# A planner that writes the order of one kernel: its price list and three of its waiting times are changed

## Chip, cores and metric

The kernel runs on one core of a Trainium2 chip. The metric is device time of one execution in microseconds (us), lower is better. TensorE (PE), VectorE (DVE), ScalarE (ACT) and GpSimd (POOL) each work through their own list of instructions in the order in which the program wrote them; SyncE (SP) issues nearly all DMAs, in order as well.

## What is computed

Two macaron layers over 256 latent tokens and 256 context tokens of width 1024, all in float32. Cut to what matters:

```python
for i in range(2):                                  # layer 0: DeltaNet mixer, layer 1: window attention
    mx = silu(c) @ ada_w[i] + ada_b[i]              # nine vectors of 1024 for the latent tokens
    mc = silu(c_ctx) @ ada_w[i] + ada_b[i]          # nine for the context tokens
    x   = x   + 0.5 * gate * swiglu(rms_norm(x) * scale + shift)       # FFN 1, width 2816
    ctx = ctx + 0.5 * gate * swiglu(rms_norm(ctx) * scale + shift)
    x   = x   + gate * mixer(norm(x), norm(ctx))    # chunked gated DeltaNet in two directions, or attention
    ctx = ctx + gate * mixer(...)                   # not in the last layer
    x   = x   + 0.5 * gate * swiglu(norm(x))        # FFN 2; for ctx not in the last layer
    ctx = ctx + 0.5 * gate * swiglu(norm(ctx))
```

Shift, scale and gate are the nine vectors `mx`, `mc`, called the ada vectors below.

## The kernel before

Activations lie transposed: features on partitions, 512 tokens (context in columns 0 to 255, latent in 256 to 511) on the free axis. A weight block of 128x128 times an activation block is done as three matmuls (`mm3`): high part times high part, high times low, low times high, since every float32 is split into a rounded part and a remainder. ACT and DVE (or POOL) make these splits from weights that SP loads into the rings `raw` and `ub` of two tiles each. A ring `u` of 76 tiles of 128x512 holds all else: a tile is given back after its last use in the program.

An FFN has three parts of 6, 8 and 8 hidden blocks (`self.parts`): pairs of products, then `out_blocks`, which adds the gated result to `X` block by block. The last part of an FFN computes the last four blocks in two halves, context columns first, and each half is followed by `norm_half`: a sum of squares over partitions on PE (`rstd`, a matmul with `ones`), then eight chunks of the next input `H` by DVE, ACT and POOL (`h_chunks`). The next stage begins with the context halves of four units, so that the latent norm can run meanwhile.

The ada vectors are a background task (`ada_gen`): a vector is 16 steps, each of which loads 256 KB of `ada_w` and multiplies and adds it into accumulators on DVE, ACT and POOL; after the 16th, four matmuls with `ones1` sum over partitions, ACT copies the result, PE transposes it. Tiles are loaded three steps ahead. During DeltaNet the task is paused (`ada_pause`, set before the last `out_blocks` of the first FFN, cleared when the norm after DeltaNet is made). `need(l, v)` runs the task at once if a vector is asked for that isn't there.

In DeltaNet (`deltanet`) PE works through projections, while `dn_prep`, `dn_solve` (a triangular solve on DVE), `dn_kq` (sums of squares of the queries, then products of keys and queries) and `dn_chain` (eight recurrent steps per head) run as tasks, heads 0 to 3 first, then 4 to 7. For the second group `dn_kq` stores keys and queries to DRAM, and `dn_group` loads them again when the first group is through.

**The planner.** The order on all engines is written while the program is built, by `Sched`. It keeps a clock that each matmul moves on by its assumed duration (`mm`, `tr`), estimated times at which DVE, ACT and POOL come free (`note`), and for each piece of a tile when it will be ready. A task is a generator: what it yields is the time in ns until it wants to go on, and `yield self.at(tile)` means "when the tile is ready by the estimate". What a task then issues stands at that place in every engine's list. The estimates are used only for the order: on the chip an instruction waits until its inputs are truly there, and with it all that stands behind it on its engine.

Of the kernel before, what the change touches and what calls it, by code (L numbers as in the profile page):

```python
# [68 lines left out]
class Sched:  # L69
# [3 lines left out]
    def __init__(self):  # L73
        self.clock = 0.0
        self.tasks = []
        self.busy = False
        self.free = {"vector": 0.0, "scalar": 0.0, "gpsimd": 0.0, "dma": 0.0}
        self.ready = {}
        self.slot = 0.0

    @staticmethod
# [15 lines left out]
    def note(self, eng, ins, outs, n, extra):  # L97

        t = max(self.free[eng], self.when(*ins))
        a, b, c = {"vector": (70.0, 1.04, 65.0), "scalar": (60.0, 0.84, 90.0), "gpsimd": (80.0, 2.15, 0.0)}[eng]  # L100
        self.free[eng] = t + a + b * n + c * extra
        for o in outs:
            self.mark(o, self.free[eng] + 150.0)

# [109 lines left out]
class Kernel:  # L214
    PACE = 2450.0
    Z0 = 1
# [32 lines left out]
    def at(self, *aps):  # L249

        return max(0.0, self.s.when(*aps) - self.s.clock)


    def act(self, **kw):
# [13 lines left out]
    def mm(self, out, lhsT, rhs, start=True, stop=True, tp=None, ns=None):  # L268
        kw = {} if tp is None else {"tile_position": tp}
        if ns is None:  # L270
            n = 1
            for d in rhs.shape[1:]:
                n *= d
            m = lhsT.shape[-1]
            if lhsT.dtype == F32R:
                ns = max(107.0, n / 2.4)
            else:
                ns = max(214.0 if m > 64 else 135.0, 4 * n / 2.4)
        self.s.product([lhsT, rhs], out, ns)
        self.nc.tensor.matmul(out, lhsT, rhs, start=start, stop=stop, **kw)  # L280
        self.s.tick(ns)

    def tr(self, out, in_, k=128):
        self.s.product([in_], out, 107.0)
        self.nc.tensor.transpose(out, in_, self.ident[:k, :k])  # L285
        self.s.tick(107)

# [390 lines left out]
    def ada_gen(self, todo, pace):  # L678
# [12 lines left out]
        def ahead(i):  # L691
            if i < len(steps) and i not in tiles and not (self.ada_pause and steps[i][3:] == (0, 0)):
                if not self.ada_pause or i - 1 in tiles or i - 1 == cur[0]:
                    fetch(i)
# [6 lines left out]
        for i, (l, v, conds, h, k) in enumerate(steps):  # L701
# [30 lines left out]
            p = c = None  # L732
            yield (1800.0 if i < 16 else pace) - (self.s.clock - t0)
            if h == 1 and k == 7:
                yield self.at(*acc.values())
                n = 32 * 2 * len(conds)
# [6 lines left out]
                self.act(out=sb[0:n, :], in_=ps[0:n, :], func=AF.Copy)  # L743
                yield self.at(sb)
                p2 = self.cht()
# [106 lines left out]
    def norm_half(self, hf, sq, l, slot):  # L852
        self.need(l, 3 * slot)
        self.need(l, 3 * slot + 1)
        sl = CTX if hf == "c" else LAT
        yield self.at(self.acc[:, sl]) + self.margin
        yield from self.rstd(sl, sq)
        yield self.at(self.rs[:, sl])
        yield from self.h_chunks(hf, l, slot, range(8), 300)
        if hf == "x":  # L860
            self.tables("silu")
            self.norming = self.urgent = self.lo_mix = False
            if (l, slot) == (0, 2):
                self.ada_pause = False

# [228 lines left out]
    def ffn(self, l, j, sl, nxt, start=False):  # L1094
        v = 8 if j else 2
        for pi, (p0, n) in enumerate(self.parts):
            self.G = ([], [])
            if pi == 0:
                if start:
# [56 lines left out]
    def dn_consts(self):  # L1156
        nc, a = self.nc, self.a
        self.dnc = [self.u(), self.u()]
        for i in range(2):
            nc.sync.dma_start(out=self.dnc[i], in_=a["dnc"][:, 512 * i:512 * i + 512])  # L1160
        d0, d1 = self.dnc
        self.tri = [d0[:, 0:128], d0[:, 128:256]]
        self.bones = d0[:, 256:384]
        self.tric = [d0[:, 384:448], d0[:, 448:512]]
        self.hsel = [d1[:, 0:128], d1[:, 128:256]]
        self.maskr = self.const([128, 2, 64], "maskr", F32R)
        self.identr = self.const([128, 128], "identr", F32R)
        self.fwd, self.bwd = d1[:, 384:385], d1[:, 385:386]
        rows = self.u()
# [323 lines left out]
    def dn_kq(self, g):  # L1493

        while any(4 * g + i not in self.qsq for i in range(4)):
            yield 500
        yield self.at(*[self.qsq[4 * g + i] for i in range(4)])
        yield from self.dn_ss(self.qsq, g, self.lnq)
# [43 lines left out]
    def dn_chain(self, h):  # L1542
# [8 lines left out]
        for s, (q, e) in enumerate(self.STEPS):  # L1551
# [9 lines left out]
            if s:  # L1561
                for i in range(2):
                    self.mm(ps[half[i], 0:128], kT[:, c0[i]:c0[i] + 64], S[:, e ^ i, :], ns=135)
                yield self.at(ps[:, 0:128])
# [18 lines left out]
            if s:  # L1583
                for i in range(2):
                    self.mm(po[half[i], 0:128], qT[:, c0[i]:c0[i] + 64], S[:, e ^ i, :], ns=135)
            self.mm(po[:, 128:256], KQ, w)
# [286 lines left out]
    def att_worker(self, todo):  # L1873
        nc = self.nc
        while todo:
# [44 lines left out]
            for k in range(4):  # L1920
                for par in range(2):
                    self.mm(po[64 * par:64 * par + 64, 0:128], self.aV[c][:, 128 * k + 64 * par:128 * k + 64 * par + 64],
                            PT[par][:, 128 * k:128 * k + 128], start=(k == 0), stop=(k == 3), ns=135)
            hi, lo = self.OH[0][u][:, qs], self.OH[1][u][:, qs]
# [38 lines left out]
    def run(self, upto=None):  # L1963
# [5 lines left out]
        self.margin = 300.0  # L1969
        self.lo_pool = self.ada_pause = self.norming = self.urgent = self.lo_mix = False  # L1970
        self.plan_weights()
# [61 lines left out]
```

## Time and profile before

| what | value |
|---|---|
| median of 3 runs | 1926.43 us (1924.85 to 1928.46) |
| the profiled execution | 1927.54 us, span of its instructions 1925.8 us |
| PE busy | 1866.0 us, 97% of the span |
| DVE, ACT, POOL busy | 1283.1, 965.7, 649.2 us |
| DMA | 271.76 MB, mean 141 GB/s |

Rows of the trace give times from the start of the span. A line of code is that of a helper for nearly all instructions (L280 is the matmul in `mm`, L285 the transpose, L184 the wrapper of the other engines), so tiles tell them apart: `mm` is a PSUM tile, `u`, `ub`, `raw`, `big` are tiles of the rings, `ones` the matrix of ones of either sum.

### The profile page before, as it was taken

To read this page: it belongs to the slowest core of one execution; us is meant where nothing else is said; L and a number is where in the kernel's file an instruction comes from. 1 tells how busy PE (TensorE), PEld (TensorE's weight loads), DVE (VectorE), ACT (ScalarE), POOL (GpSimd) and SP (SyncE) were. 2 spreads that over 40 slices of the span, in tenths; PEclk is the share of its full clock that TensorE was granted. 3 is DMA by queue.
4 is the path that set the end of the run, shared out by engine and by line. 5 is a ranking of instruction groups with operands and counts; after the bars stand their busy time and mean duration, and the time that the engine had idled before them with its cause. 6 is when DMAs were issued, how large, how long until landed. Compare 5 with 4: busy or idle time off the path is not lost.

```text
span 1925.8 us, 28970 instructions
## 1 busy us (share of the span) xinstructions
PE 1866.0 (97%) x10719; PEld 1527.8 (79%) x10719; DVE 1283.1 (67%) x2121; ACT 965.7 (50%) x2106; POOL 649.2 (34%) x597
## 2 busy tenths in 40 slices
PE   8999999999999999999999999999999999899998
PEld 5878788887777766787888888888888889678887
DVE  4897878855986975478888655743333345966665
ACT  4545535457466555465454344641322348865653
POOL 3344434453545535354444224420000047330000
PEclk8999999999999999999999999999999999999999
DMA  9655554423222252444555555433223325124761
GB/s 293 209 198 201 181 186 170 139 63 108 90 68 88 67 182 83 145 169 152 197 191 197 186 172 173 153 126 109 88 88 109 113 69 123 47 67 148 235 197 66
DMA packets 238421, 271.76 MB, mean 141 GB/s; under 512 B 12184, under 2 KB 188592, under 8 KB 238280
## 3 DMA queue, kind: packets, MB, share of 16 engines
q1 hardware_dynamic: 237415, 269.22, 43.0%
q8 instruction: 84, 1.38, 0.3%
q10 hardware_dynamic: 720, 0.59, 0.1%
q14 instruction: 58, 0.47, 0.1%
q0 software_dynamic: 144, 0.11, 0.0%
HBM read 259.39 MB, written 10.49 MB: 140 GB/s over the span
## 4 chain that ended last, share of the span: by engine, by line
PE 56%; DVE 7%; ACT 3%; issue 3%; POOL 1%; DMA 1%; POOLq 0%; DVEq 0%; ACTq 0%; SPq 0%
PE mm L280 55%; DVE u L184 6%; ACT u L184 3%; PE mm L285 1%; POOL u L184 1%; DVE st L184 0%; DVE big L184 0%; DMA u<-ZD 0%; DMA u<-XD 0%; ACT L184 0%; DVE ub L184 0%; POOLq L184 0%; ACT sc L184 0%; DVEq L184 0%; ACTq L184 0%
## 5 line engine op out<-in xcount | busy, mean ns | idle before, releaser
L280 PE MATMUL mm<-u 128*128 128x512 f32 (+4 forms) x9496 | 1782.0, 353 | 22.4 <-POOL u L184 8.3
L280 PEld LDWEIGHTS mm<-u 128*128 128x128 f32 (+1 forms) x9496 | 1459.3, 184 | 325.8 <-issue 42.3
L184 POOL TENSOR_TENSOR u<-u 128x512 f32<-128x512 f32 (+4 forms) x389 | 430.2, 1112 | 909.8 <-ACT u L184 859.0
L184 ACT ACTIVATE u<-u 128x512 fp32r<-128x512 f32 (+8 forms) x361 | 171.2, 485 | 441.9 <-DVE u L184 420.3
L184 ACT ACTIVATE u<-mm 128x128 f32<-128x128 f32 (+3 forms) x382 | 151.9, 412 | 291.7 <-PE mm L280 223.1
L184 DVE TENSOR_TENSOR u<-raw,u 128x512 fp32r<-128x512 f32 (+2 forms) x270 | 218.6, 851 | 65.1 <-ACT u L184 65.0
L184 DVE SCALAR_TENSOR_TENSOR u<-u,cc 128x512 f32<-128x512 f32 x196 | 229.2, 1170 | 4.2 <-DMA u<-in_ada_w 1.0
L184 DVE TENSOR_TENSOR u<-ub,u 128x512 fp32r<-128x512 f32 x252 | 198.1, 830 | 26.7 <-ACT u L184 26.4
L184 ACT ACTIVATE u<-raw 128x512 fp32r<-128x512 f32 (+1 forms) x372 | 205.8, 607 | 14.6 <-DMA raw<-in_ffn_w 10.3
L184 ACT ACTIVATE u<-u,cc 128x512 f32<-128x512 f32 x224 | 151.9, 711 | 84.9 <-DMA u<-in_ada_w 71.7
L184 POOL TENSOR_TENSOR u<-raw,u 128x512 fp32r<-128x512 f32 x98 | 130.1, 1351 | 141.5 <-ACT u L184 121.8
L184 ACT ACTIVATE u<-ub 128x512 fp32r<-128x512 f32 (+1 forms) x282 | 155.9, 608 | 20.2 <-DVE u L184 8.2
L184 DVE TENSOR_TENSOR u<-u,mm 128x512 f32<-128x512 f32 x66 | 45.2, 685 | 164.9 <-PE mm L280 156.7
L184 DVE TENSOR_TENSOR u<-u 128x512 fp32r<-128x512 f32 (+5 forms) x155 | 96.9, 626 | 64.9 <-ACT u L184 61.9
L184 DVE SCALAR_TENSOR_TENSOR u<-mm,mod,u 128x256 f32<-128x256 f32 x168 | 74.5, 477 | 93.8 <-PE mm L280 93.6
L184 DVE SCALAR_TENSOR_TENSOR u<-u,mod 128x256 f32<-128x256 f32 (+1 forms) x140 | 88.3, 683 | 23.9 <-ACT u L184 23.6
L184 ACT ACTIVATE u<-u,mod 128x256 fp32r<-128x256 f32 (+1 forms) x124 | 56.0, 501 | 52.7 <-DVE u L184 52.3
L184 DVE SCALAR_TENSOR_TENSOR u<-mm,cw,u 128x510 f32<-128x510 f32 (+1 forms) x96 | 71.3, 743 | 9.6 <-ACT u L184 7.9
L285 PE MATMUL mm<-ident,u 128*128 128x128 f32 (+3 forms) x361 | 55.3, 289 | 13.7 <-DVE u L184 7.1
L184 DVE TENSOR_TENSOR u<-mm,u 128x256 f32<-128x256 f32 (+2 forms) x102 | 41.6, 419 | 36.5 <-PE mm L280 16.6
L285 PEld LDWEIGHTS mm<-ident,u 128*128 128x128 f32 (+3 forms) x361 | 43.7, 149 | 25.2 <-ACT u L184 6.0
L280 PE MATMUL mm<-u,ones 128*32 128x512 f32 (+2 forms) x172 | 37.3, 546 | 13.0 <-DVE u L184 8.9
(116 smaller groups left out, 587.0 us busy)
## 6 DMA issues: line engine op xcount, KB each, us to landing
u<-in_ada_w SPq DMA_DIRECT2D x256, 256.0 KB, 5.7
ub<-in_ffn_w SPq DMA_DIRECT2D x60, 1024.0 KB, 5.3
raw<-in_ffn_w SPq DMA_DIRECT2D x58, 1024.0 KB, 5.3
raw<-in_dn_w_in SPq DMA_DIRECT2D x16, 1024.0 KB, 5.7
ub<-in_ada_w SPq DMA_DIRECT2D x12, 512.0 KB, 7.2
ub<-in_ffn_w SPq DMA_DIRECT2D x6, 768.0 KB, 4.7
raw<-in_ffn_w SPq DMA_DIRECT2D x6, 768.0 KB, 4.8
raw<-in_dn_w_out SPq DMA_DIRECT2D x4, 1024.0 KB, 5.8
```

The costliest lines, as they stand in the source:

```text
L184: r = f(*a, **k)
L280: self.nc.tensor.matmul(out, lhsT, rhs, start=start, stop=stop, **kw)
L285: self.nc.tensor.transpose(out, in_, self.ident[:k, :k])
```

## The change

The price list of the planner gets other numbers (`Sched.note`, `mm`, `tr`), a vector operation with two inputs is lengthened by 45% of the time for which POOL is still busy by the estimate, and a matmul after a switch to fewer than 128 rows or columns gets 95 ns more (`form`). A new wait `spare` is `at` plus 2500 ns; it stands before the sums and the transposes of an ada vector and before the sums in `dn_kq`. The latent half of `norm_half` waits 1200 ns after its estimate where it waited 300. `PACE`, the time of an ada step, goes from 2450 to 2650 ns (1800 to 1900 for the first vector). From the last part of the first FFN on, `ada_hold` keeps the first tiles of a new vector from being loaded ahead. The constants of DeltaNet, two `u` tiles, are split: what is used to the end goes to a tile of its own (`keep`), the rest is last used in `dn_gates`.

```diff
+        self.split = False
+    def form(self, split):
+        was, self.split = self.split, split
+        return 95.0 if split and not was else 0.0
...
-        self.free[eng] = t + a + b * n + c * extra
+        took = a + b * n + c * extra
+        if eng == "vector":
+            both = len(ins) > 1 and not any(i.tensor.name.startswith("mm") for i in ins)
+            if both:
+                took += 0.45 * max(0.0, min(took, self.free["gpsimd"] - t))
+        self.free[eng] = t + took
         for o in outs:
-            self.mark(o, self.free[eng] + 150.0)
+            self.mark(o, self.free[eng] + 200.0)
...
-    PACE = 2450.0
+    PACE = 2650.0
...
+    def spare(self, *aps):
+        return max(0.0, self.s.when(*aps) + 2500.0 - self.s.clock)
...
             if lhsT.dtype == F32R:
-                ns = max(107.0, n / 2.4)
+                ns = n / 2.4 + m / 9.4
             else:
-                ns = max(214.0 if m > 64 else 135.0, 4 * n / 2.4)
+                ns = (214.0 if m > 64 else 107.0) * max(1.0, n / 128) + 12.0
+        ns += self.s.form(lhsT.shape[0] < 128 or lhsT.shape[-1] < 128)
...
-        self.s.product([in_], out, 107.0)
+        ns = 109.0 + self.s.form(in_.shape[0] < 128)
+        self.s.product([in_], out, ns)
...
-            if i < len(steps) and i not in tiles and not (self.ada_pause and steps[i][3:] == (0, 0)):
+            if i < len(steps) and i not in tiles and not ((self.ada_pause or self.ada_hold) and steps[i][3:] == (0, 0)):
...
-            yield (1800.0 if i < 16 else pace) - (self.s.clock - t0)
+            yield (1900.0 if i < 16 else pace) - (self.s.clock - t0)
             if h == 1 and k == 7:
-                yield self.at(*acc.values())
+                yield self.spare(*acc.values())
...
-                yield self.at(sb)
+                yield self.spare(sb)
...
-        yield self.at(self.acc[:, sl]) + self.margin
+        yield self.at(self.acc[:, sl]) + (self.margin if hf == "c" else 1200.0)
...
-                self.ada_pause = False
+                self.ada_pause = self.ada_hold = False
...
+            if pi == 2 and (l, j) == (0, 0):
+                self.ada_hold = True
...
-        self.dnc = [self.u(), self.u()]
-        for i in range(2):
-            nc.sync.dma_start(out=self.dnc[i], in_=a["dnc"][:, 512 * i:512 * i + 512])
-        d0, d1 = self.dnc
+        d0, d1 = self.u(), self.u()
+        nc.sync.dma_start(out=d0[:, 0:256], in_=a["dnc"][:, 0:256])
+        nc.sync.dma_start(out=d1[:, 0:384], in_=a["dnc"][:, 512:896])
+        keep = self.const([128, 258], "keep")
+        nc.sync.dma_start(out=keep[:, 0:256], in_=a["dnc"][:, 256:512])
+        nc.sync.dma_start(out=keep[:, 256:258], in_=a["dnc"][:, 896:898])
...
-        yield self.at(*[self.qsq[4 * g + i] for i in range(4)])
+        yield self.spare(*[self.qsq[4 * g + i] for i in range(4)])
...
-                    self.mm(ps[half[i], 0:128], kT[:, c0[i]:c0[i] + 64], S[:, e ^ i, :], ns=135)
+                    self.mm(ps[half[i], 0:128], kT[:, c0[i]:c0[i] + 64], S[:, e ^ i, :], ns=110)
...
```

Two more matmuls with `ns=135` get 110, and the views `tri`, `bones`, `tric`, `hsel`, `fwd`, `bwd` point to the new places.

## Rows read from the trace of the kernel before

**Rows 1.** Busy time by stretch; us, PE, PEld, DVE, ACT, POOL, PE clock, DMA.

```profile
45.00:365.00 320.00, 319.62 (x1454) 256.39 (x1453) 270.60 (x320) 156.23 (x278) 142.70 (x95) 1.00 0.57 192
...
895.00:1195.00 300.00, 300.00 (x1384) 243.53 (x1382) 220.63 (x282) 133.97 (x237) 112.51 (x77) 1.00 0.54 185
...
1570.00:1735.00 165.00, 149.47 (x1185) 132.35 (x1185) 113.39 (x274) 125.21 (x293) 81.28 (x77) 0.99 0.27 71
```

**Rows 2.** Waits of PE between 411 and 792 us: total us, times, longest.

```profile
PE mm L280 <- ACT u L184: 7.2, 7, 3.3
PE mm L280 <- POOL u L184: 3.6, 5, 1.0
PE mm L280 <- DVE u L184: 3.3, 7, 0.8
```

**Rows 3.** PE in order of time: start us, us, what, idle time before it.

```profile
83.75 21.01 PE L280 MATMUL mm<-u 128*128 128x512 f32 x92
104.69 1.31 PE L280 MATMUL mm<-u,ones 128*32 128x512 f32 x8
107.51 0.66 PE L285 MATMUL mm<-ident,u 128*128 128x128 f32 x4 [0.38 <-ACT u L184]
...
388.80 1.00 PE L280 MATMUL mm<-u 128*128 128x256 f32 x7
389.72 1.04 PE L280 MATMUL mm<-u,ones 128*32 128x512 f32 x2
392.97 1.06 PE L280 MATMUL mm<-u,ones 128*32 128x512 f32 x6 [2.20 <-DVE u L184]
...
396.00 0.66 PE L285 MATMUL mm<-ident,u 128*128 128x128 f32 x4 [0.83 <-ACT u L184]
...
894.15 1.06 PE L280 MATMUL mm<-u,ones 128*32 128x512 f32 x6 [1.28 <-DVE u L184]
```

**Rows 4.** PE in order of time at the first sums of `dn_kq`.

```profile
516.81 1.06 PE L280 MATMUL mm<-u,ones 128*32 128x512 f32 x6
521.15 1.23 PE L280 MATMUL mm<-u,ones 128*32 128x512 f32 x2 [3.28 <-ACT u L184]
```

**Rows 5.** Busy time by stretch where the clock was low; columns as in rows 1.

```profile
521.90:525.30 3.40, 3.40 (x11) 2.18 (x12) 3.33 (x8) 1.90 (x3) 0.00 (x0) 0.50 0.01 2
750.60:757.40 6.80, 6.80 (x40) 5.10 (x38) 4.40 (x15) 2.99 (x14) 4.35 (x8) 0.50 0.60 204
```

**Rows 6.** PE in order of time at the norms after DeltaNet and before attention.

```profile
831.55 0.67 PE L280 MATMUL mm<-u,ones 128*128 128x256 f32 x2 [1.79 <-DVE u L184]
...
832.77 11.62 PE L280 MATMUL mm<-u 128*128 128x256 f32 x94
844.88 5.29 PE L280 MATMUL mm<-u 128*128 128x256 f32 x42 [0.50 <-POOL u L184]
...
1585.16 0.67 PE L280 MATMUL mm<-u,ones 128*128 128x256 f32 x2 [1.78 <-DVE u L184]
```

**Rows 7.** DVE by shape, 60 to 365 us: count, busy us, mean ns.

```profile
L184 DVE TENSOR_TENSOR u<-raw,u 128x512 fp32r<-128x512 f32 x54 | 53.7, 1034 | 2.9 <-ACT u L184 2.9
```

**Rows 8.** The same, 1740 to 1900 us, where POOL does nothing.

```profile
L184 DVE TENSOR_TENSOR u<-raw,u 128x512 fp32r<-128x512 f32 x55 | 35.9, 687 | 38.4 <-ACT u L184 38.4
```

**Rows 9.** PE between the two groups of DeltaNet.

```profile
683.49 1.07 PE L280 MATMUL mm<-u,ones 128*32 128x512 f32 x8
...
694.49 0.75 PE L280 MATMUL mm<-ub,u 32*32 32x32 f32 x64 [0.48 <-ACT u L184]
...
748.97 10.06 PE L280 MATMUL mm<-u 64*128 64x128 f32 x64 [1.63 <-ACT u L184]
```

**Rows 10.** SP's queue there: start us, us, what it issued.

```profile
686.84 0.42 SPq L184 DMA_DIRECT2D QD<-u  x1
```

**Rows 11.** SP and DVE in order of time around the first vector after DeltaNet.

```profile
838.39 2.92 SPq L184 DMA_DIRECT2D u<-in_ada_w  x6
...
908.17 0.86 DVE L184 SCALAR_TENSOR_TENSOR u<-mm,mod,u 128x256 f32<-128x256 f32 x2
```

More of the change, by code (lines that the diff above doesn't have):

```diff
@@ L283, in tr @@
     def tr(self, out, in_, k=128):
-        self.s.product([in_], out, 107.0)
+        ns = 109.0 + self.s.form(in_.shape[0] < 128)
+        self.s.product([in_], out, ns)
         self.nc.tensor.transpose(out, in_, self.ident[:k, :k])
-        self.s.tick(107)
+        self.s.tick(ns)
     def mm3(self, ps, w, h, nk, sl=ALL, ks=None, start=True, stop=True):
@@ L1157, in dn_consts @@
         nc, a = self.nc, self.a
-        self.dnc = [self.u(), self.u()]
-        for i in range(2):
-            nc.sync.dma_start(out=self.dnc[i], in_=a["dnc"][:, 512 * i:512 * i + 512])
-        d0, d1 = self.dnc
+        d0, d1 = self.u(), self.u()
[4 more added lines that the diff above has]
+        nc.sync.dma_start(out=keep[:, 256:258], in_=a["dnc"][:, 896:898])
         self.tri = [d0[:, 0:128], d0[:, 128:256]]
-        self.bones = d0[:, 256:384]
-        self.tric = [d0[:, 384:448], d0[:, 448:512]]
+        self.bones = keep[:, 0:128]
+        self.tric = [keep[:, 128:192], keep[:, 192:256]]
         self.hsel = [d1[:, 0:128], d1[:, 128:256]]
@@ L1167, in dn_consts @@
         self.identr = self.const([128, 128], "identr", F32R)
-        self.fwd, self.bwd = d1[:, 384:385], d1[:, 385:386]
+        self.fwd, self.bwd = keep[:, 256:257], keep[:, 257:258]
         rows = self.u()
@@ L1584, in dn_chain @@
                 for i in range(2):
-                    self.mm(po[half[i], 0:128], qT[:, c0[i]:c0[i] + 64], S[:, e ^ i, :], ns=135)
+                    self.mm(po[half[i], 0:128], qT[:, c0[i]:c0[i] + 64], S[:, e ^ i, :], ns=110)
             self.mm(po[:, 128:256], KQ, w)
@@ L1922, in att_worker @@
                     self.mm(po[64 * par:64 * par + 64, 0:128], self.aV[c][:, 128 * k + 64 * par:128 * k + 64 * par + 64],
-                            PT[par][:, 128 * k:128 * k + 128], start=(k == 0), stop=(k == 3), ns=135)
+                            PT[par][:, 128 * k:128 * k + 128], start=(k == 0), stop=(k == 3), ns=110)
             hi, lo = self.OH[0][u][:, qs], self.OH[1][u][:, qs]
@@ L1969, in run @@
         self.margin = 300.0
-        self.lo_pool = self.ada_pause = self.norming = self.urgent = self.lo_mix = False
+        self.lo_pool = self.ada_pause = self.ada_hold = self.norming = self.urgent = self.lo_mix = False
         self.plan_weights()
```

## The prediction

> **What bounds the kernel now.** I read the busy time by stretch first. In the FFN stretches from 45 to 365 and from 895 to 1195 us PE is busy for 319.6 of 320 and 300.0 of 300 us [rows 1]; the order of time shows 92 matmuls of 512 columns in 21.01 us, 228 ns each [rows 3]. No order makes these stretches shorter: the number of matmuls doesn't change. So the change can win only where PE stands still: in DeltaNet, in the joints between stages and in attention, where PE lacks 15.5 of 165 us [rows 1]. The waits of PE say for what: between 411 and 792 us 7.2 us for ACT, 3.6 for POOL and 3.3 for DVE [rows 2]. Then I looked up each place in the order of time. What the reader is to see there: PE's list is worked off in order, so an instruction put too early holds up everything behind it, though the matmuls behind it need nothing from it. That is what a planner that is too hopeful does.
>
> How hopeful it is, one pair of rows shows. The same subtraction (two inputs in SBUF, 128x512) takes 1034 ns on average while POOL has work [rows 7] and 687 ns in the last FFN, where POOL does nothing [rows 8]. The planner before reckons 70 + 1.04 x 512 = 602 ns for both. Its 512-column matmul is 213 ns, 228 on the chip.
>
> **Term A, sums of the ada vectors.** Four times PE waits at the end of a vector: 0.38 us before a transpose, 2.20 and 0.83 us at 390 and 396, 1.28 us at 894 [rows 3]; together 4.69 us. The other vectors show no such wait. Behind the waiting matmul stand the matmuls of the FFN, which are ready; put off, the sums let them go first, and the work in front of them is free. At 390 the first sums ran at 389.72 and the rest at 392.97 [rows 3]: 3.25 us too early, against 2.5 us of delay. Of that wait I leave 0.4 us and count **4.3 us**. Bounds: nothing, if the sums meet another late accumulator, and 4.7.
>
> How much of the contention the new price list sees is a second question. For one subtraction it adds up to 0.45 x 602 = 271 ns; the rows differ by 1034 - 687 = 347 ns on average, and that average holds operations that POOL left alone. The Trainium skill (SBUF — State Buffer, Who interferes with whom) says that a vector operation with two SBUF inputs and a GpSimd operation that reads SBUF exclude each other for a whole instruction. By that rule the loser pays the whole rest of the other's instruction and not 45% of it, and one more late operation of some 0.3 us would stay at each of the four places, so that A would be about 3.1 us; the sum goes without it.
>
> **Term B, the sums of the queries.** At 516.81 us three quarters of the sums run, and the last quarter waits until 521.15, 3.28 us idle, for ACT behind a DVE that is busy with the solver [rows 4]. It is 4.3 us too early; the delay is 2.5, and dearer DVE operations and 50 ns more per result push it further. I leave 1.0 us and count 2.3. Right behind that wait the granted clock is 0.50, that is 1.2 GHz, from 521.9 to 525.3 [rows 5]: the 3.4 us would hold the same work in 1.7 at 2.4 GHz. I count them, since PE then has no wait of 3 us there: B is **4.0 us**. Bounds 0 (the clock falls anyway and the wait is as long) and 5.0. Nobody waits for these sums soon: the products of `dn_kq` also wait for the decay factors.
>
> **Term C, the latent norm.** At 831.55 PE waits 1.79 us for the last accumulation [rows 6], and 1.78 us at the joint before attention [rows 6]. Put off by 900 ns more, PE would do context matmuls meanwhile. But these are done too soon anyway: after the norm's sums PE has 11.62 us of them, and at 844.88 it waits another 0.50 us for the last chunk of `H` from POOL [rows 6]. The chunks hang on the end of the accumulation, not on PE, so what is gained at 831 is waited out at 844: **0**. Bounds: +3.6 if the chunks come sooner, and -1.8 if the delay overshoots at both joints and starts the chunks 0.9 us later. Before the last FFN only latent tokens are left, PE has nothing else in its list, and the delay changes no order: 0.
>
> **Term D, pace and hold.** From 104.69 to 389.72 six vectors end [rows 3], 47.5 us each. The new step is 2650 ns; the old 2450 ns of a clock that counts 213 ns for a matmul of 228 were 2450 x 228 / 213 = 2622 real. So 16 steps take 0.4 us more, and the two delays 5.0: 52.9 us per vector. From 107 us on, the sixth vector then ends at about 107 + 5 x 52.9 = 372, plus some 3 us for a first tile that is no longer loaded ahead. The pause begins with the last `out_blocks`. At 388.80 PE is in its 256-column halves [rows 3], and before these come four blocks of 24 matmuls at 228 ns, 21.9 us: the pause begins before 367. So the seventh vector, which ended at 390, is put off until after DeltaNet. It is needed there by the first addition at 908.17, and started at 838.39 it needs 53 us [rows 11]: ready near 897. Cost 0, covered by 11 us; beyond that its price is a rival below. The vectors of layer 1 are not needed before 1195 us; nine of 53 us from 897 on end near 1374, the two for the next norm near 1003.
>
> **Term E, the rest of the price list.** DeltaNet's other waits are those of rows 2 without the 3.28 us of B: 10.8 us. Where other matmuls are ready, a later place fills them; where a chain of small steps is all there is, as in attention and at the end of a group, it does nothing. I take a quarter, **2.5 us**, and 0 for attention. Bounds: all of it and a low-clock stretch as at 750.6 [rows 5] (half of 6.8 us), 14 us; and below, a chain that gets its turn later, the rival below. The two tiles and the split constants: two more small DMAs on SP during the last `out_blocks`, where only weights follow, 0; tiles given back early matter only if the ring is short, for which I found no wait that says so.
>
> **Sum.** 4.3 + 4.0 + 0 + 0 + 2.5 = 10.8 us from the profiled execution's 1927.5, which stands 1.1 us above the median: 1926.4 - 10.8 = **1916 us**.
>
> **Rivals.**
> *The second group starts late (slower).* The sums at 683.49 get the same delay. The stores of keys and queries come right behind their products, from 686.84 on [rows 10], then the loads, and the chains of the second group need these. Until 695.2 PE's list holds the solver's small matmuls, which wait for DVE and ACT [rows 9]. If sums and products fall behind them, stores and loads move by 695.2 - 683.5 = 11.7 us. Three units of 24 matmuls, 16.4 us, can fill the hole, but they are then missing between the chain's steps, where PE already waits 1.63 us at 748.97 [rows 9] and runs at half clock after it [rows 5]. Full price 11.7 + 3.4 = 15.1 us: 1931 us. For it: PE's list there is written by tasks alone. Against: the solver's estimate moves later as well, by dearer DVE operations, and the sums may keep their place. It decides from about 14.7 us on (10.8 and the 3.9 of the bound).
>
> *The waits only move (no change).* What stands behind a sum may wait for the same late engine, as in term C: then A and B return at the next evacuation, 1924 to 1928 us. Against it: behind the sums at 390 and 894 the FFN matmuls start at once.
>
> *The late vector.* If the seventh vector isn't there at the first addition, `need` runs its last steps at once: two operations of 0.7 to 1.0 us [rows 7, 8], the sums, ACT's copy and the transposes in a row, some 5 us: 1921 us. It needs 11 us more than worked out.
>
> *More gained.* If half of DeltaNet's remaining waits go, with one of the low-clock stretches, E is 5.4 + 3.4 = 8.8: 1910 us; with C's 3.6 it is 1906.
>
> **Chances.** Forecast (1909 to 1922) 0.52; more gained 0.14; the late vector 0.08; no change 0.12; second group late 0.14. A change of 0.2%, 3.9 us, is about what a measurement of this kernel can tell from none. The first three are faster: 0.74; no change 0.12; slower 0.14. For 8 in 10 the range goes from 1904 (more gained) to 1930 (short of the full price of the late group).
>
> **What would show it.** In the profile after: no idle time before the ones-sums of the vectors and of the first `dn_kq`, and no stretch of clock 0.50 near 522; six vectors before DeltaNet and ten after it, ends 53 us apart; the wait before the norm's sum gone and a longer one before the last chunk; the FFN stretches as long as before. Wrong I would be if the stores QD come more than 5 us after the sums at that place, if a vector's sum stands right before the first gated addition after DeltaNet with PE idle, or if PE's rows in the dense FFN stretches show waits that rows 1 don't have.

## The result, and the profile after

The changed kernel takes 1938.72 us (median of 9 runs, 1931.4 to 1945.83), the kernel before 1926.43: a ratio of 1.0067, 95% interval 1.0044 to 1.0089. It is 12.3 us slower; 1916 was predicted. The profiled execution took 1945.19 us, near the top of its runs, so the trace below accounts for 17.6 us of span and the medians for 12.3. The runs of this order lie further apart than those of before (14 us against 6).

The page after has PE 11 us busier with as many matmuls, and a 7 and an 8 in its clock line, from 680 to 777 us (a slice is 48.6 us), and one more 8 in attention:

```profile
span 1943.4 us, 29009 instructions
...
PE 1877.0 (97%) x10719; PEld 1535.0 (79%) x10719; DVE 1292.9 (67%) x2124; ACT 969.3 (50%) x2108; POOL 641.7 (33%) x594
...
PEclk9999999999999978999999999999999999899999
```

To see where the time went I cut the span at the sums of the latent norm that opens each stage (the two `ones` matmuls of 256 columns, as in [rows 6]):

| stretch, us | before | after |
|---|---|---|
| start to the norm before DeltaNet | 420.9 | 413.1 |
| DeltaNet | 410.7 | 436.0 |
| FFN 2 of layer 0 | 380.7 | 377.2 |
| FFN 1 of layer 1 | 372.9 | 371.9 |
| attention | 139.0 | 144.9 |
| last FFN | 201.6 | 200.3 |

The FFN stretches win 13.6 us together; DeltaNet loses 25.3 and attention 5.9. Busy time by stretch, columns as in [rows 1], for before (DeltaNet, attention):

```profile
420.90:831.60 410.70, 390.43 (x3024) 302.11 (x3024) 291.17 (x587) 238.20 (x669) 199.55 (x250) 0.98 0.32 103
...
1587.00:1725.90 138.90, 128.90 (x1050) 113.82 (x1048) 96.59 (x245) 105.85 (x252) 66.89 (x63) 1.00 0.30 77
```

and for after:

```profile
413.10:849.10 436.00, 406.27 (x3026) 308.41 (x3025) 295.73 (x585) 240.05 (x670) 196.02 (x250) 0.94 0.30 97
...
1598.20:1743.10 144.90, 133.71 (x1050) 117.23 (x1049) 96.01 (x245) 107.09 (x254) 68.34 (x64) 0.96 0.29 74
```

PE does the same matmuls in DeltaNet (3024 and 3026). It stands still for 436.0 - 406.3 = 29.7 us where it was 20.3, and takes 15.8 us more for the work itself, at a mean clock of 0.94 for 0.98. DeltaNet has 51 us at 0.50 in this trace and 20 in that of before; 31 us more at half clock cost an estimated 15.5. So the loss is two things: 9.5 us of new waits, and 15.8 us more for the same work, about as much as the clock explains. In attention it is 1.2 and 4.8 us.

Where in DeltaNet this comes in, five stretches show: up to the first addition to the state by the first chain (heads 0 to 3), that chain, from its last addition to the first one of the second chain (heads 4 to 7), the second chain, the rest. Before:

```profile
420.90:587.30 166.40, 157.41 (x1191) 127.02 (x1191) 123.22 (x212) 104.37 (x263) 81.37 (x78) 0.97 0.30 91
587.30:674.30 87.00, 85.08 (x548) 61.40 (x549) 73.12 (x160) 52.77 (x156) 47.77 (x68) 1.00 0.22 71
674.30:708.30 34.00, 30.99 (x491) 22.37 (x489) 27.36 (x60) 20.03 (x65) 13.33 (x23) 1.00 0.73 254
708.30:769.30 61.00, 58.45 (x423) 41.10 (x423) 33.20 (x96) 30.55 (x104) 30.54 (x52) 0.94 0.20 68
769.30:831.60 62.30, 58.49 (x377) 50.21 (x376) 34.26 (x64) 30.47 (x83) 26.54 (x32) 0.97 0.40 135
```

After:

```profile
413.10:599.50 186.40, 170.11 (x1237) 133.45 (x1235) 136.56 (x223) 115.12 (x281) 87.41 (x84) 0.98 0.28 86
599.50:694.20 94.70, 89.48 (x806) 63.55 (x804) 79.55 (x172) 54.41 (x163) 45.98 (x68) 0.95 0.37 118
694.20:720.90 26.70, 23.50 (x190) 16.95 (x181) 10.79 (x32) 10.37 (x42) 6.73 (x16) 0.74 0.30 107
720.90:790.60 69.70, 66.54 (x429) 45.08 (x430) 37.43 (x100) 31.21 (x106) 31.45 (x52) 0.85 0.18 57
790.60:849.10 58.50, 56.63 (x381) 49.38 (x381) 31.40 (x60) 28.93 (x81) 24.45 (x31) 1.00 0.43 145
```

The first chain's first addition comes 20.0 us later and the chain takes 7.7 us more; the stretch between the chains is 7.3 us shorter, the second chain takes 8.7 us more, the rest 3.8 less. The new idle time lies ahead of the first chain (16.3 us for 9.0) and in it (5.2 for 1.9); between the chains PE stands still as long as before (3.2 and 3.0). There and in the second chain the clock is what is new: 0.74 and 0.85, for 1.00 and 0.94. Ahead of the first chain 32 more matmuls of 512 columns run, 7.3 us at 228 ns:

```profile
L280 PE MATMUL mm<-u 128*128 128x512 f32 x437 | 109.3, 403 | 0.0
...
L297 PE MATMUL mm<-u 128*128 128x512 f32 x469 | 115.9, 401 | 0.0
```

With the 7.3 us of waits that is 14.6 of the 20.0 us; the traces give no place for the rest.

These stretches answer to [rows 1], the third again the one around attention:

```profile
45.00:350.00 305.00, 304.73 (x1385) 247.19 (x1382) 245.85 (x297) 145.29 (x258) 127.58 (x85) 1.00 0.57 190
910.00:1210.00 300.00, 300.00 (x1397) 245.92 (x1398) 236.86 (x290) 136.91 (x244) 113.19 (x77) 1.00 0.53 180
1585.00:1755.00 170.00, 154.00 (x1174) 134.79 (x1173) 113.13 (x275) 125.46 (x293) 81.63 (x77) 0.95 0.27 69
```

PE's order of time in the changed kernel, at the places of [rows 3], [rows 4], [rows 6] and [rows 9]:

```profile
362.52 1.06 PE L297 MATMUL mm<-u,ones 128*32 128x512 f32 x8
...
513.08 1.06 PE L297 MATMUL mm<-u,ones 128*32 128x512 f32 x8
...
518.18 0.86 PE L303 MATMUL mm<-ident,u 128*128 128x128 f32 x4 [1.16 <-ACT u L196]
...
677.68 4.50 PE L297 MATMUL mm<-u 128*128 128x128 f32 x26 [2.00 <-DVE u L196]
682.11 1.94 PE L297 MATMUL mm<-u,ones 128*32 128x512 f32 x8
...
693.95 0.32 PE L297 MATMUL mm<-ub,u 32*32 32x32 f32 x15 [1.19 <-ACT u L196]
696.68 0.90 PE L297 MATMUL mm<-ub,u 32*32 32x32 f32 x49 [2.41 <-issue]
...
699.85 16.48 PE L297 MATMUL mm<-u 128*128 128x128 f32 x79 [0.79 <-DVE u L196]
...
761.25 13.51 PE L297 MATMUL mm<-u 64*128 64x128 f32 x64 [1.29 <-ACT u L196]
...
849.10 0.59 PE L297 MATMUL mm<-u,ones 128*128 128x256 f32 x2
...
862.36 3.86 PE L297 MATMUL mm<-u 128*128 128x256 f32 x30 [0.73 <-POOL u L196]
...
908.85 1.07 PE L297 MATMUL mm<-u,ones 128*32 128x512 f32 x8
```

What to see: the sums of the vectors (362.52, 908.85), of the queries (513.08) and of the norm (849.10) all run without a wait. From 674 to 708 us, where DeltaNet changes from its first group to the second, PE has no projection, that is no matmul with 128x128 weights and 512 columns: it has the end of the first chain, the sums of the queries, the second solver and the small products behind it, with waits of 2.00, 1.19 and 2.41 us. In the kernel before the longest such stretch at this place is 12.0 us. A row of the order of time has the shape of its first matmul and counts others of the same line and tiles with it, so the 79 at 699.85 are not all small: by shape, 18 matmuls of 512 columns run between the chains, and 45 in the kernel before:

```profile
L297 PE MATMUL mm<-u 128*128 128x512 f32 x18 | 6.2, 478 | 0.0
...
L280 PE MATMUL mm<-u 128*128 128x512 f32 x45 | 12.6, 410 | 0.0
```

Two of the low-clock stretches, by stretch:

```profile
696.40:710.10 13.70, 12.63 (x102) 9.01 (x103) 6.28 (x16) 5.07 (x22) 3.29 (x8) 0.50 0.43 160
761.30:778.40 17.10, 17.10 (x83) 11.44 (x84) 8.96 (x29) 4.61 (x20) 4.57 (x8) 0.50 0.35 112
```

SP's queue, to compare with [rows 10]:

```profile
676.41 0.42 SPq L196 DMA_DIRECT2D QD<-u  x1
...
695.82 2.82 SPq L196 DMA_DIRECT2D u<-KD  x4
```

### The profile page after: what moved, and what is told of

Same layout as the page of the kernel before. It is cut to its first block, busy times and chain, and to the rows that moved or that the text cites. A ratio compares the mean times of both kernels' runs of the same rounds, so it can differ in the third digit from the quotient of the medians.

```text
span 1943.4 us, 29009 instructions
## 1 busy us (share of the span) xinstructions
PE 1877.0 (97%) x10719; PEld 1535.0 (79%) x10719; DVE 1292.9 (67%) x2124; ACT 969.3 (50%) x2108; POOL 641.7 (33%) x594
## 5 line engine op out<-in xcount | busy, mean ns | idle before, releaser
L297 PE MATMUL mm<-u 128*128 128x512 f32 (+5 forms) x9480 | 1789.0, 356 | 26.2 <-POOL u L196 9.1
L297 PEld LDWEIGHTS mm<-u 128*128 128x128 f32 (+2 forms) x9480 | 1464.2, 186 | 335.8 <-issue 50.0
L196 POOL TENSOR_TENSOR u<-u 128x512 f32<-128x512 f32 (+4 forms) x386 | 425.2, 1107 | 924.3 <-ACT u L196 858.6
L196 ACT ACTIVATE u<-mm 128x128 f32<-128x128 f32 (+5 forms) x382 | 152.2, 413 | 274.6 <-PE mm L297 201.3
L196 DVE TENSOR_TENSOR u<-raw,u 128x512 fp32r<-128x512 f32 (+2 forms) x270 | 226.2, 879 | 63.0 <-ACT u L196 62.1
L196 DVE SCALAR_TENSOR_TENSOR u<-u,cc 128x512 f32<-128x512 f32 x196 | 223.4, 1140 | 12.8 <-DMA u<-in_ada_w 9.8
L303 PE MATMUL mm<-ident,u 128*128 128x128 f32 (+3 forms) x361 | 59.2, 297 | 20.1 <-ACT u L196 9.8
L196 DVE SCALAR_TENSOR_TENSOR u<-u,aS,mm 128x128 f32<-128x128 f32 x96 | 31.5, 345 | 24.9 <-PE mm L297 20.8
```

Of the source, the lines that this page charges most:

```text
L196: r = f(*a, **k)
```

## The experiments

In all of them the times are medians with the ratio to the kernel before and its interval. "First chain" and "second chain" are the recurrent steps of heads 0 to 3 and 4 to 7, from the first to the last addition to the state on DVE (`u<-u,aS,mm`, 48 a group); "loads" are those of the second group. Their places are us after the norm sum that opens DeltaNet. The table at the end has all of them. No kernel with the waits but without the two tiles given back early was tried.

**e1_prices and e2_waits: the price list alone, all but the price list.** The first is the kernel before with the new numbers of `note`, `mm`, `tr` and the new paces, the second the changed kernel with the old numbers of `note`, `mm`, `tr`:

```diff
-            if both:
-                took += 0.45 * max(0.0, min(took, self.free["gpsimd"] - t))
-            self.mark(o, self.free[eng] + 200.0)
+            self.mark(o, self.free[eng] + 150.0)
-                ns = n / 2.4 + m / 9.4
+                ns = max(107.0, n / 2.4)
...
```

> The kernel before with the new price list and the new ada pace alone: no spare, no hold, no longer margin, the constants as before. Theory A (the dearer vector operations give the solver its turns later, so the chains start late, PE runs out of projections and its clock falls): DeltaNet, from the latent norm's sum before it to the one after it, stays at some 436 us (before 411), and without the waits' gain in the FFNs the time is 1938 to 1946 us. Rival B (the new waits and the postponed vector do it, the price list is harmless): DeltaNet 408 to 414 us, 1922 to 1930 us.

> The changed kernel with the old price list: spare, hold, margin, pace and split constants stay. Theory A: DeltaNet 407 to 413 us, the FFN stretches keep their gain of 8 to 13 us, 1910 to 1918 us. Rival B: DeltaNet near 436 us, 1932 to 1940 us. Rival C (any new order moves DeltaNet by 10 us or more, whatever was changed): DeltaNet anywhere from 400 to 440.

Measured: prices alone 1950.11 (1.0122 [1.0104, 1.0139]), the rest alone 1921.72 (0.9982 [0.9972, 0.9991]). The loss is the price list's: 23.7 us alone (with the new paces, which e2 has too), 17.0 on top of the rest. DeltaNet is 429.5 and 412.8 us, near what theory A said; both times are 4 us above its ranges.

**e3_novec: the changed kernel with the old vector prices.**

```diff
-        if eng == "vector":
...
-            self.mark(o, self.free[eng] + 200.0)
+            self.mark(o, self.free[eng] + 150.0)
```

> The changed kernel with the old price of vector operations (no contention term, 150 ns to the result), the new prices of matmuls kept. In the first solver's stretch of DVE's list stand 32 products of the convolution; 40 in the changed kernel, 36 before. Theory A: the first solver ends sooner, the chains start sooner, DeltaNet 405 to 415 us, 1910 to 1920 us. Rival B, and a rival that blames the matmul prices: DeltaNet stays near 436 us, 1932 to 1942 us.

Measured: 1942.22 (1.0083 [1.0070, 1.0096]). Undoing the vector half mends nothing. The first chain now starts at 163 us (186 in the changed kernel), yet the second starts at 304: the loads are there only at 305.

**e4_lag4000: the solver's steps get their turn sooner**, 4000 ns before the planner thinks DVE free, where it was 800.

```diff
-        self.solve_lag = 800.0
+        self.solve_lag = 4000.0
```

> The changed kernel with one number more: the solver's steps may be issued 4000 ns before the planner thinks DVE is free (solve_lag 800 before), which leaves 32 products of the convolution in the first solver's stretch of DVE's list instead of 40; all prices stay new. Theory A: the first solver ends some 6 us sooner (8 products of 0.74 us), DeltaNet 420 to 430 us, 1924 to 1934 us. Rival B: no change against the changed kernel, 1936 to 1942 us.

Measured: 1947.25 (1.0105 [1.0090, 1.0120]), slower than both theories said. The first chain starts at 169 us instead of 186, yet it ends at 283, the loads are there at 314 and the second chain starts at 316. So theory A, that the solver gets its turns too late, is not the whole cause.

**e5_gate: projections of the second group held back** until heads 0 to 3 have done their first step.

```diff
+            if (kind, g) == (2, 1):
+                s.until(lambda: all(self.step.get(h, -1) >= 0 for h in range(4)))
+                units(2, (4, 5, 6, 7))
+                continue
```

> The changed kernel, all its prices kept, with one wait of the program: the last three groups of projections (values, queries and gates of heads 4 to 7) are issued only after the first recurrent step of heads 0 to 3. In PE's list 411 matmuls of 512 columns then stand between the gates' first matmul and that step; 449 in the changed kernel, 426 before. Theory A2 (the new prices put projections ahead of the first group's chain; the chain ends later, and then no projection is left to cover the start of the second): the first state update comes 165 to 175 us after the norm's sum instead of 186, DeltaNet 412 to 424 us, 1917 to 1930 us. Rival (the chains themselves have become slower, by their own dearer matmuls and the clock): the start moves but the end doesn't, DeltaNet 430 us or more, 1935 us or more.

Measured: 1941.15 (1.0081 [1.0067, 1.0095]). The edit did its part, the first chain starts at 180 us instead of 186 and ends at 245 instead of 281. But the loads now come at 304 instead of 292, and the second chain starts at 306, where it was 308. One leg was taken away and the other took its place: "too many projections ahead of the first chain" is not the whole cause either.

**e6_no_kq and e11_kq_first_group: the spare time before the queries' sums.** Both have the old prices; e6 takes the spare out for both groups, e11 for the second alone.

```diff
-        yield self.spare(*[self.qsq[4 * g + i] for i in range(4)])
+        yield self.at(*[self.qsq[4 * g + i] for i in range(4)])
```

> The kernel with the old price list and the new waits, less the spare before the queries' sums. If that spare gained what the prediction's term B says, this is 3 to 6 us slower than with it (1921.7): 1924 to 1928 us, with PE idle for 3 us before the last sum and the clock low behind it. If the place only changed hands, 1920 to 1923 us.

> The kernel with the old price list and the new waits, the spare before the queries' sums for heads 0 to 3 only (for both groups 1921.7 us, for none 1913.3). If the first group's wait does the damage by moving all that follows it in the lists, 1920 to 1924 us; if the second group's does, by delaying the stores and loads of keys and queries, 1911 to 1915 us.

Measured: 1913.31 (0.9939 [0.9925, 0.9952]) without it, 1926.85 (1.0004 [0.9995, 1.0013]) with it in the first group alone, 1921.72 in both (e2). e6 is faster than either of its expectations. So the spare costs 8.4 us where it was to bring 4, and the first group's is the one that costs. In order of time PE shows why the wait it removes is no gain. Without it (e6):

```profile
511.54 1.04 PE L285 MATMUL mm<-u,ones 128*32 128x512 f32 x2 [3.22 <-ACT u L184]
```

With it (e2):

```profile
512.26 1.05 PE L285 MATMUL mm<-u,ones 128*32 128x512 f32 x2 [0.53 <-ACT u L184]
...
517.45 2.06 PE L290 MATMUL mm<-ident,u 128*128 128x128 f32 x8 [2.79 <-ACT u L184]
```

3.22 us before the sums became 0.53 there and 2.79 before the transposes behind them: 3.32. And the first chain, which starts at 164 and 163 us, ends at 258 instead of 250: more matmuls of 512 columns run inside it, 174 in e6 and 195 in e2, 4.8 us at 228 ns.

```profile
L285 PE MATMUL mm<-u 128*128 128x512 f32 x174 | 47.2, 407 | 0.9 <-POOL u L184 0.6 <-ACT u L184 0.3
...
L285 PE MATMUL mm<-u 128*128 128x512 f32 x195 | 53.6, 414 | 0.0
```

**e7_no_margin: e2 with the old margin of the latent norm.**

```diff
-        yield self.at(self.acc[:, sl]) + (self.margin if hf == "c" else 1200.0)
+        yield self.at(self.acc[:, sl]) + self.margin
```

> The kernel with the old price list and the new waits, less the longer margin before the latent norm's sum. Term C of the prediction (worth nothing, since the chunks hang on the accumulation): 1920 to 1923.5 us, PE idle 1.8 us before these sums and less before the last chunk. If the margin costs something, 1917 to 1920 us; if it gains, 1924 to 1926 us.

Measured: 1923.88 (0.9993 [0.9980, 1.0007]); e2 had 0.9982 [0.9972, 0.9991], and the intervals overlap. At the joint after DeltaNet e7 has PE wait as before:

```profile
828.01 0.67 PE L285 MATMUL mm<-u,ones 128*128 128x256 f32 x2 [1.81 <-DVE u L184]
...
841.36 4.82 PE L285 MATMUL mm<-u 128*128 128x256 f32 x38 [0.49 <-POOL u L184]
```

and e2 has it wait 0.71 and 0.26 us for POOL on either side of sums that wait for nothing:

```profile
826.57 0.62 PE L285 MATMUL mm<-u 128*128 128x256 f32 x3 [0.71 <-POOL u L184]
827.02 0.59 PE L285 MATMUL mm<-u,ones 128*128 128x256 f32 x2
...
838.25 1.30 PE L285 MATMUL mm<-u 128*128 128x256 f32 x6 [0.26 <-POOL u L184]
```

That is 1.3 us in the trace (2.30 against 0.97), too little for these runs.

**e8_old_in_mixers and e12_best: the changed kernel with the old prices during DeltaNet and attention alone**; e12 has `at` before the queries' sums as well.

```diff
+        self.s.old = True
         self.attention((1, 2))
+        self.s.old = False
...
-            if both:
+            if both and not self.old:
...
-                ns = n / 2.4 + m / 9.4
+                ns = max(107.0, n / 2.4) if self.s.old else n / 2.4 + m / 9.4
```

> The changed kernel with the old price list inside DeltaNet and attention only, the new one in all FFNs. If the whole loss lies in the order of the mixers, DeltaNet is 409 to 414 us, attention 138 to 141, the FFN stretches as in the changed kernel (413, 377, 372), 1913 to 1920 us. If the FFN's prices cost something at the joints, 1922 us or more.

> The changed kernel with the old price list inside DeltaNet and attention and no spare before the queries' sums. From the sections of the other runs: 413 or 414 to the norm before DeltaNet, 405 DeltaNet, 377, 372, 139, 200: 1906 to 1912 us. If the latent norm's sections don't add up so, 1913 to 1916.

Measured: 1919.34 (0.9968 [0.9956, 0.9979]) and 1913.28 (0.9928 [0.9916, 0.9940]). The old prices inside the two mixers alone bring 19.4 us against the changed kernel, so that is where the new ones cost. In the FFNs the new prices do no harm; FFN 1 of layer 1 takes 372.4 us with them and 375.3 with the old ones and the waits (e2, e6). e12 and e6 are the fastest orders of all and don't differ by more than their intervals.

**e9_vec_only, e10_pe_only, e15_after_no_kq: which half of the price list.** e9 is e6 with the new numbers of `note`, e10 e6 with those of `mm` and `tr`. e15 is the changed kernel with `at` before the queries' sums and so has both halves.

```diff
+        ns += self.s.form(lhsT.shape[0] < 128 or lhsT.shape[-1] < 128)
...
```

> The kernel with the new waits but none before the queries' sums (1913.3 us with the old price list), and of the new price list the vector half alone: contention term and 200 ns to the result. In PE's list 498 matmuls of 512 columns then stand ahead of the first recurrent step, 422 with the old list. Theory A2 (what counts is how many projections stand ahead of the first chain): the first group ends 17 us later (76 matmuls of 0.227 us), its end and not the second solver sets the second group's start, DeltaNet 420 to 432 us, 1928 to 1940 us. Rival E (only the matmul half costs): DeltaNet 403 to 409 us, 1911 to 1916 us.

> The same base with the matmul half alone (durations, the 95 ns after a switch, the ns of the chain's matmuls). 400 matmuls ahead of the first step, 422 with the old list. Theory A2 in its full form (the two groups compete: a first chain that gets ahead puts off the second group's keys, products and loads): the first chain is early, the second solver and the stores of keys and queries are 15 us late, DeltaNet 424 to 434 us, 1932 to 1942 us. Theory A2 in its simple form (fewer projections ahead is better): DeltaNet below 405 us, 1905 to 1912 us.

> The changed kernel without the spare before the queries' sums. If the spare costs the same 8 us with the new prices as with the old ones: 1930 to 1932. If the projections that stand ahead of the first chain set the end of it anyway: 1937 to 1941, no change from the changed kernel.

Measured: none of the halves 1913.31, vector half 1923.48 (0.9988 [0.9978, 0.9998]), matmul half 1943.78 (1.0094 [1.0073, 1.0115]), both 1936.95 (1.0053 [1.0030, 1.0075]). They don't add up: by the table below the second chain waits for the end of the first chain in e9 and e15, and for the loads in e10. DeltaNet by stretch, in e6,

```profile
413.40:818.80 405.40, 386.60 (x3026) 298.41 (x3025) 290.04 (x585) 238.08 (x669) 198.66 (x250) 0.99 0.33 105
```

in e9,

```profile
411.80:829.00 417.20, 395.23 (x3032) 304.07 (x3031) 296.17 (x585) 240.42 (x672) 199.16 (x250) 0.97 0.31 102
```

and in e10:

```profile
413.30:846.00 432.70, 396.33 (x3018) 301.82 (x3018) 297.15 (x587) 238.98 (x669) 197.43 (x250) 0.97 0.30 98
```

PE stands still for 18.8, 22.0 and 36.4 us. In PE's list 422 matmuls of 512 columns of DeltaNet stand ahead of the first recurrent step in e6, 498 in e9, 400 in e10. With the vector half the first chain starts at 186 us instead of 163 and ends at 270 instead of 250. With the matmul half it is as early as in e6, but the second group's solver starts at 202 instead of 182 and its loads land at 305 instead of 286. Between the chains 45 matmuls of 512 columns run in e6, 19 in e9 and 114 in e10:

```profile
L285 PE MATMUL mm<-u 128*128 128x512 f32 x45 | 13.7, 437 | 0.0
...
L291 PE MATMUL mm<-u 128*128 128x512 f32 x19 | 6.1, 458 | 0.0
...
L292 PE MATMUL mm<-u 128*128 128x512 f32 x114 | 28.8, 400 | 0.0
```

**e13_col_only, e14_pe_without_col, e16_after_without_col: one number of the matmul half**, the price of a 32-bit matmul: e6 with it, e10 without it, the changed kernel without it.

```diff
-                ns = max(107.0, n / 2.4)
+                ns = n / 2.4 + m / 9.4
```

> The kernel with the old prices and no spare before the queries' sums (1913), plus one number: a 32-bit matmul is reckoned at n / 2.4 + m / 9.4 ns, 227 ns for 512 columns in place of 213. The theory that this number does it, since it moves the planner's clock against every matmul that carries the work and so against every due time: 1940 to 1945 like the whole matmul half, second chain near 70 us, attention near 145. Rival, the switch to split tiles and the small products do it: 1911 to 1918, chain near 60, attention 139 to 140.

> The same base plus the other numbers of the matmul half: 95 ns for a switch to split tiles, 109 ns for a transpose, 12 ns more for small products. Theory (the 512-column price does it): 1911 to 1918, second chain near 60 us, attention 139 to 140. Rival (the switch and the small products do it): 1940 to 1945. If both this and the run with the one number come out slow, each alone is enough.

> The changed kernel with the 32-bit matmul reckoned as before, 213 ns for 512 columns, all other new prices kept. Theory (this number does it): the second chain back near 60 us and attention at 139 to 140; DeltaNet then costs what the vector half and the spare cost, 1925 to 1932. Rival (the other numbers do it): 1936 to 1942.

Measured: 1946.39 (1.0108 [1.0087, 1.0129]), 1936.00 (1.0055 [1.0037, 1.0073]), 1942.62 (1.0084 [1.0067, 1.0101]). Each alone is enough: 33 us by the one number, 23 by the others, and taking the one out of the changed kernel mends nothing. The theory of one guilty number falls. But the two parts do not do the same: with the one number (e13) the second chain takes 62.6 us and the loads land at 313, without it (e14, e16) the second chain takes 69.9 and 70.1 us and the loads land at 291 and 286. A second chain near 70 us, which the theory had laid to the one number, comes with the others.

All kernels, us; PE idle is that of DeltaNet, the span of the stage less PE's busy time; "512 between" counts the matmuls with 128x128 weights and 512 columns between the two chains:

| kernel | median | DeltaNet | PE idle | first chain ends | loads land | second chain starts | 512 between | attention |
|---|---|---|---|---|---|---|---|---|
| e6 | 1913.3 | 405.4 | 18.8 | 250 | 286 | 284 | 45 | 139.9 |
| e12 | 1913.3 | 409.7 | 18.6 | 252 | 288 | 286 | 45 | 139.4 |
| e8 | 1919.3 | 415.5 | 23.4 | 259 | 289 | 291 | 24 | 139.4 |
| e2 | 1921.7 | 412.8 | 22.6 | 258 | 288 | 292 | 24 | 139.9 |
| e9 | 1923.5 | 417.2 | 22.0 | 270 | 276 | 296 | 19 | 139.4 |
| e7 | 1923.9 | 415.5 | 20.9 | 258 | 288 | 291 | 24 | 139.9 |
| before | 1926.4 | 410.7 | 20.3 | 253 | 289 | 287 | 45 | 139.0 |
| e11 | 1926.9 | 416.9 | 22.7 | 256 | 290 | 289 | 24 | 139.4 |
| e14 | 1936.0 | 423.9 | 26.8 | 256 | 291 | 293 | 46 | 143.2 |
| e15 | 1937.0 | 430.8 | 27.2 | 278 | 287 | 306 | 18 | 145.1 |
| after | 1938.7 | 436.0 | 29.7 | 281 | 292 | 308 | 18 | 144.9 |
| e5 | 1941.2 | 432.6 | 29.0 | 245 | 304 | 306 | 118 | 145.2 |
| e3 | 1942.2 | 434.7 | 36.8 | 249 | 305 | 304 | 114 | 145.5 |
| e16 | 1942.6 | 437.3 | 32.0 | 280 | 286 | 307 | 19 | 139.6 |
| e10 | 1943.8 | 432.7 | 36.4 | 249 | 305 | 302 | 114 | 145.2 |
| e13 | 1946.4 | 436.8 | 38.8 | 258 | 313 | 311 | 98 | 145.1 |
| e4 | 1947.3 | 441.1 | 35.1 | 283 | 314 | 316 | 24 | 142.0 |
| e1 | 1950.1 | 429.5 | 27.3 | 277 | 284 | 305 | 18 | 141.4 |

The rule in it: the second chain starts no earlier than 3 us before the loads land and no earlier than 26 us after the end of the first chain, and within 7 us of the later of these two. From its last recurrent step to the next norm it is 57 to 64 us in every kernel. The end of the second solver fits as a third bound: the second chain starts no earlier than 11 us behind it, and in e6, e12, e13 and before just that, so there the loads and the solver can't be told apart. What does not order the kernels is the work left between the chains: with 114 or 118 matmuls (e3, e5, e10) they are as slow as with 18 (e1, e15, after).

## Why the prediction was wrong

**Term A came true at its places, and is small.** No sum or transpose of a vector waits any more at the four places where [rows 3] had 0.38, 2.20, 0.83 and 1.28 us. The rule cited from the Trainium skill (SBUF — State Buffer, Who interferes with whom) gave 3.1 us, with 0.3 us left at each of the four; in this trace nothing is left, though no run has these waits alone, and no median tells 3.1 from 4.3 us. The kernel with all but prices and the queries' spare (e6) gains 13.1 us where A, C and D were to bring 4.3. In its trace 7.5 us of the gain lie before the norm that opens DeltaNet, 5.3 in DeltaNet, 3.9 in FFN 2 of layer 0 and 1.7 in the last FFN; 2.4 are lost in FFN 1 of layer 1 and 0.9 in attention. Which edit does which was not taken apart.

**Term B had the wrong sign.** At its place it came true: the changed kernel's sums at 513.08 have no wait, the longest behind them before 560 us is 1.16 us, and the clock is 1.00 there. The step that failed is "Nobody waits for these sums soon". With the old prices the wait went from the sums to the transposes behind them (e2), and the first group's chain ends 8 us later for it; 8.4 us is what it costs (e6, e11). With the new prices it costs 1.8 us (e15 against the changed kernel), within the runs' scatter; there the first chain is late anyway.

**Term C: 0, and the runs can't tell it from 0.** The trace has 1.3 us.

**Term D was right.** Six vectors end before DeltaNet, the last at 362.52 (372 was reckoned), and ten behind it, the first at 908.85; no addition waits for a late vector.

**Term E is the step that failed.** "Where other matmuls are ready, a later place fills them" was put at +2.5 us; it is -17 us on top of e2 and -24 on top of e6 (e15). (A quarter of its 10.8 us is 2.7, and [rows 2] leaves out 5.1 us of smaller waits there; neither changes the outcome.) It took the price list to move waits one by one. But in DeltaNet the list decides how projections, the only work that needs no chain, are dealt out between two groups, and when each group's chain ends and its loads land. Dearer vector operations put off every step of the first group, and projections run in its place: 498 ahead of it instead of 422 in e9, whose first chain ends 20 us later. Dearer matmuls bring the first group's steps forward in the list (400 ahead in e10) and push back the second group's projections, and with them its solver and its loads, by 20 and 19 us. Either way the second chain starts later. In the changed kernel it starts 21 us later than before, behind a first chain that ends 28 us later; longer waits and more matmuls of 512 columns ahead of that chain make 14.6 of the 20 us by which it starts later, and the time at half clock costs more than the new waits (about 15.5 and 9.5 us). That the waits bring on the low clock is likely and not shown.

**The rival "second group starts late"** named the right stage and sign, and its 1931 us was nearer than the forecast; that was luck. Its mechanism was not what happened: the stores were issued at 676.41 us, ahead of the sums at 682.11, not behind them, and the loads landed 16 us before the second chain's first addition. By the rule of the table the second chain followed the end of the first, 26 us behind it. "A chain that gets its turn later", named as a bound of E, is nearer to it, but carried neither a price nor a chance of its own. Of the three signs that were named for being wrong none appears: the stores come ahead of the sums, no vector's sum holds up the first gated addition, and PE misses 0.3 of 305 and 0.0 of 300 us in the dense FFN stretches.

What stays open: why attention takes 141 to 146 us with most forms of the matmul half and 139 to 140 without it (e16 has part of that half and takes 139.6), and why a dearer 512-column matmul alone makes the loads land 27 us later (e13 against e6). The prices change the place of nearly every task, and I found no single move that does it.

## What to carry to other kernels

A planner's prices are knobs of a search and not only estimates: the new price of a 512-column matmul, 227 ns, is nearer to the measured 228 than the old 213, and alone costs 33 us. So don't value a new price list by the waits it might fill; look at when each group's chain ends and its loads land, and try prices and waits as separate edits, by stage. The work left between two groups is no measure by itself. A wait removed in front of a chain is only a gain if the instruction behind it doesn't need the same late engine, and if what runs in its place doesn't put off the chain. And a row of the order of time can hold several shapes: ask for them by shape before calling it one kind of work.

## What the runs showed of the hardware

The granted clock stayed at 0.50, 1.2 GHz, for 17.1 us from 761.3 us on although PE was busy for 17.10 of these 17.10 us, with the chain's small products; before it PE had waited 1.29 us. At 696.4 it lasted 13.7 us with 12.63 busy, after waits of 1.19 and 2.41 us. In the FFN stretches, also without idle time but with matmuls of 512 columns, the clock is 1.00 throughout. Not every wait is followed by a low clock: the solver's 2.39 us at 571.63 in the same trace lie in a stretch at 1.00.

```profile
571.63 0.38 PE L297 MATMUL mm<-ub,u 32*32 32x32 f32 x22 [2.39 <-issue]
...
566.70:614.10 47.40, 40.85 (x421) 28.87 (x410) 29.71 (x60) 30.67 (x76) 21.83 (x30) 1.00 0.22 73
```

What the low clock costs shows in the second chain, which has 0.6 us more idle time: 429 matmuls in 69.7 us at a mean of 0.85, where before 423 took 61.0 us at 0.94.
